# Fourteen more floats in a table of constants: where the tiles of a transformer block start in SBUF

## The chip, the cores and the metric

The kernel runs on one core of one Trainium2 chip. The metric is device time in microseconds (us) of one execution of the whole program. The kernel before was timed three times: 1037.11, 1038.47 and 1039.26 us, so its median is 1038.47 us. One more execution, of 1039.65 us, was recorded by the hardware profiler; all rows below come from that one.

## The reference, cut to what matters

One transformer block over 1024 tokens of width 1024, all in float32, and a last normalisation:

```python
h = rms_norm(x, norm_mix)
proj = h @ w_in                              # 1024 x 1536: 16 query heads, 4 key and 4 value heads of 64
mix = sliding_window_sink_attention(...)     # window 128, blocks of 128, alibi slopes, one sink per head
x = x + mix @ w_out                          # 1024 x 1024
gu = rms_norm(x, norm_ffn) @ w_gate_up       # 1024 x 5632
x = x + (silu(gu[:, :2816]) * gu[:, 2816:]) @ w_down
return rms_norm(x, final_norm)
```

Nearly all arithmetic is in four matrix products: with `w_in`, `w_out`, `w_gate_up` and `w_down`. The constants that the change is about are three small ones per partition: the exponent -0.5 for the reciprocal roots, two copies of the 16 sinks (as they are and negated), and a scale for the queries.

## The kernel before, in words

**Precision.** Every large operand is held as two float32r halves, hi (a rounded copy, made by ScalarE) and lo (the rest, a subtraction on VectorE or GpSimd). A product is three matmuls: hi with hi, hi with lo, lo with hi. A matmul has a moving operand, 128 partitions by up to 512 columns, and a stationary one, 128 by 128, which a weight load (LDWEIGHTS, engine PEld in the views) brings in ahead of it.

**Stages.** The program is one order of work written out by hand; each engine has its queue, and helpers (`Stream`, `Queue`) count matmuls and put the other engines' steps between them.

- 0 to 100 us: x is normalised and transposed into `HH` (`store`, L138); the value projection `v_mm` (L362, results in `VV`); the first half of the key and query projection (`gemm_steps`, L251), moving `HH`, stationary `wc`.
- 100 to 276 us: 32 attention units (`Unit`, L441): scores L470 and L471 (stationary `qt`, moving `KH`, `KL`), exponentials, transposes L505, values L519 (stationary `VV`, moving `pr`). Between them run the second half of L251 and then the output projection L696 (stationary `HH`, which now holds the attention output; moving `wc_o`).
- 276 to 370 us: the rest of attention and of the output projection (L732, L1073), the second normalisation, and its transposes into `HH` and `HT`.
- 370 to 808.6 us: gate and up products (`product`, L1060) in seven Strassen products for each of 22 column blocks: stationary `ws`, moving `HH` or `HT`, in groups of 12 matmuls.
- 808.6 to 987.3 us: the down projection, again in Strassen products (`d_product`, L1343): both operands are slots of `HH`, which by now holds activations and down weights; results are added into `acc`.
- 987.3 us to the end: the last columns of it, plain (L1426, both operands in `HH`), and the final norm.

**Where tiles start.** SBUF is laid out when the program is built. Pools grow from the low end (`const`, `hpool`, `vpool`, `early`, `att`, `ht`, `accp`) or, with `side="right"`, from the high end (`rows`, `wp`, `kpool`, `gp`). A tile's place is rounded up to 32 bytes. Start addresses in each partition, and what is left after division by 64:

| tile | start, bytes | remainder |
|---|---|---|
| `ident`, `small` (168 bytes, takes 192) | 16512, 17024 | 0, 0 |
| `HH` | 17216 | 0 |
| `VV`, `HT`, `acc` (the lowest of each) | 82752 | 0 |
| `wv` and the first half's `qst` | 99136, 115520 | 0 |
| attention's `dist`, `t`, `pr` | 99136, 101184, 113856 | 0 |
| `KH`, `KL` | 130912, 147296 | 32 |
| `raw_g`, `raw_s`, `sum`, `p1` (pool `gp`) | 132960 and up | 32 |
| weights: raw tiles, `wc`, `ws`, `wd` (pool `wp`) | 163680 and up | 32 |
| rows: x, `xr`, `xn`, `qt`, `gate`, `up`, `y` of the norms | 200544 and up | 32 |

Every slice that a matmul reads lies a multiple of 512 bytes from its tile's start, so the tile's remainder is the operand's. The pairs (moving, stationary) are therefore: L251 and L1060 (0, 32); L696, L732 and L1073 (32, 0); L362, L519, L1343 and L1426 (0, 0); L470 and L471 (32, 32).

The lines that the change touches are L74 to L76: the tile `small` and its slices.

Of the kernel before, what the change touches and what calls it, by code (L numbers as in the profile page):

```python
# [9 lines left out]
F32 = mybir.dt.float32  # L10
# [6 lines left out]
P = 128  # L17
# [5 lines left out]
NH = 16  # L23
# [9 lines left out]
def trunk_kernel(  # L33
# [31 lines left out]
    const = ctx.enter_context(tc.tile_pool(name="const", bufs=1))  # L65
# [5 lines left out]
    psa = ctx.enter_context(tc.tile_pool(name="psum_a", bufs=4, space=PSUM))  # L71

    ident = const.tile([P, P], F32, name="ident")
    small = const.tile([P, 2 + 2 * NH + 8], F32, name="small")  # L74
    sink_bc, sink_neg = (small[:, 2 + i * NH : 2 + (i + 1) * NH] for i in range(2))
    qscale = small[:, 2 + 2 * NH :]  # L76
    HH = hpool.tile([P, 4, 2, NK, 2 * P], F32R, name="HH")
    q_dram = [[dram.tile([P, 4, G, P], F32, name=f"qs_{i}_{kv}") for kv in range(NKV)] for i in range(2)]
    x2_dram = [dram.tile([P, D], F32, name=f"x2s_{t}") for t in range(NT)]
# [1388 lines left out]
```

## Time and profile before

| what | us |
|---|---|
| median of three runs | 1038.47 |
| profiled execution | 1039.65 |
| its span, first to last instruction | 1037.9 |
| PE (TensorE) busy with matmuls | 1000.8 (96%) |
| DVE (VectorE) busy | 643.1 (62%) |
| ACT (ScalarE) busy | 454.8 (44%) |
| POOL (GpSimd) busy | 588.9 (57%) |

A busy time is the union of the times in which an engine's instructions ran. Matmuls overlap: one is shown from its first column going in to its last result, while the next starts before that. So the time that one matmul costs is the distance between two starts, its pitch, and not its duration: a piece of the timeline with N matmuls of one kind lasts N pitches and a tail, the duration of one less its pitch. Pieces of the chain of waits have no such tail.

### The profile page before, as it was taken

The page shows a single profiled execution, that of the slowest core. Times are in us where ns is not written, and L with a number is a line of the kernel's source. Part 1 is how long each engine was busy: PE and PEld are TensorE (multiplying, and loading weights), DVE is VectorE, ACT ScalarE, POOL GpSimd, SP SyncE. Part 2 cuts the span into 40 slices and gives each one's busy share as a digit, 9 for nine tenths or more (in the row PEclk, how much of TensorE's full clock was granted, in tenths as well). Part 3 has the DMA queues.
Part 4 walks back from the last instruction along what each step waited for, and adds up shares of the span by engine and source line. Part 5 has one row for each costly group of instructions (what it writes and reads, how often), then busy time and mean ns, then how long its engine had stood idle before and what let it go on. Part 6 is the DMA issues. An engine that isn't in the chain of part 4 may idle for free.

```text
span 1037.9 us, 13830 instructions
## 1 busy us (share of the span) xinstructions
PE 1000.8 (96%) x4740; PEld 826.4 (80%) x4740; DVE 643.1 (62%) x1070; ACT 454.8 (44%) x955; POOL 588.9 (57%) x557
## 2 busy tenths in 40 slices
PE   7999999999978799999999999999999899999997
PEld 7888888888866598888888888888788688888885
DVE  5421687778886585554555455555644468886774
ACT  5533777777845443323323323323323443343334
POOL 4633555565354452663763753754743968988572
PEclk8999999999998999999999999999999999999999
DMA  8548655654355631313304413403324765343213
GB/s 271 135 123 212 153 164 133 164 191 122 105 160 140 185 103 61 132 45 126 134 24 137 145 28 126 151 20 133 132 102 138 274 266 184 109 145 108 85 41 122
DMA packets 98983, 138.28 MB, mean 133 GB/s; under 512 B 6368, under 2 KB 66784, under 8 KB 98912
## 3 DMA queue, kind: packets, MB, share of 16 engines
q1 hardware_dynamic: 98624, 136.61, 41.8%
q8 instruction: 37, 0.61, 0.2%
q10 hardware_dynamic: 288, 0.79, 0.2%
q14 instruction: 34, 0.28, 0.1%
HBM read 99.89 MB, written 35.39 MB: 130 GB/s over the span
## 4 chain that ended last, share of the span: by engine, by line
PE 63%; DMA 1%; POOL 1%; DVE 1%; ACT 0%; issue 0%; SPq 0%; POOLq 0%; DVEq 0%; ACTq 0%
PE d L1343 16%; PE gu_A L1060 12%; PE gu_B L1060 12%; PE gu_C L1060 12%; PE gu_D L1060 6%; PE dl L1426 4%; DMA acc<-x2s 1%; PE mo L1073 1%; DVE ws L925 0%; POOL sum L901 0%; POOL wc_oB L63 0%; POOL xr L641 0%; PE pt_b L620 0%; SPq L1311 0%; ACT wc_oB L60 0%
## 5 line engine op out<-in xcount | busy, mean ns | idle before, releaser
L1343 PE MATMUL d<-HH 128*128 128x512 f32 x756 | 174.8, 394 | 4.1 <-DVE acc L1354 4.1
L1343 PEld LDWEIGHTS d<-HH 128*128 128x128 f32 x756 | 143.7, 190 | 35.0 <-DVE acc L1354 4.5
L972 POOL TENSOR_TENSOR gate<-gate,up 128x512 f32<-128x512 f32 x33 | 50.4, 1529 | 162.5 <-issue 71.5
L1060 PE MATMUL gu_A<-HH,ws 128*128 128x512 f32 (+2 forms) x552 | 132.2, 388 | 0.0
L251 PE MATMUL pc<-HH,wc_c 128*128 128x512 f32 x480 | 122.0, 398 | 0.0
L1060 PEld LDWEIGHTS gu_A<-HH,ws 128*128 128x128 f32 x552 | 101.6, 188 | 22.9
L925 DVE TENSOR_TENSOR ws<-sum,ws 128x512 fp32r<-128x512 f32 x88 | 81.8, 939 | 60.8 <-ACT ws L921 60.7
L1241 POOL TENSOR_TENSOR HH<-raw_s,HH 128x512 fp32r<-128x512 f32 x63 | 92.1, 1479 | 41.8 <-ACT HH L1238 41.8
L251 PEld LDWEIGHTS pc<-HH,wc_c 128*128 128x128 f32 x480 | 87.3, 188 | 17.9
L921 ACT ACTIVATE ws<-raw_g 128x512 fp32r<-128x512 f32 x66 | 40.6, 627 | 129.6 <-issue 51.1
L921 ACT ACTIVATE ws<-sum 128x512 fp32r<-128x512 f32 x88 | 53.8, 626 | 96.5 <-POOL sum L901 61.2
L925 DVE TENSOR_TENSOR ws<-raw_g,ws 128x512 fp32r<-128x512 f32 x66 | 71.4, 1090 | 35.7 <-ACT ws L921 35.4
L496 POOL TENSOR_SCALAR t<-t,st 128x256 f32<-128x256 f32 (+1 forms) x128 | 62.7, 510 | 52.5 <-DVE st L494 32.4
L1238 ACT ACTIVATE HH<-raw_s 128x512 fp32r<-128x512 f32 x63 | 39.4, 625 | 85.0 <-PE d L1343 36.7
L1241 DVE TENSOR_TENSOR HH<-wd,HH 128x512 fp32r<-128x512 f32 x62 | 66.4, 1076 | 12.5 <-ACT HH L1238 12.5
L1354 DVE TENSOR_TENSOR acc<-d,acc 128x512 f32<-128x512 f32 x80 | 54.3, 686 | 31.5 <-PE d L1343 21.1
L483 ACT ACTIVATE t<-t,st 128x256 f32<-128x256 f32 (+1 forms) x128 | 61.9, 485 | 27.1 <-DVE st L475 27.1
L63 POOL TENSOR_TENSOR wc_c<-raw_c,wc_c 128x1024 fp32r<-128x1024 f32 x20 | 48.0, 2402 | 34.9 <-ACT wc_c L60 34.6
L1060 PE MATMUL gu_C<-HT,ws 128*128 128x512 f32 (+2 forms) x288 | 67.3, 381 | 0.0
L1060 PE MATMUL gu_D<-HT,ws 128*128 128x512 f32 (+2 forms) x276 | 66.4, 388 | 0.0
L1060 PE MATMUL gu_B<-HH,ws 128*128 128x512 f32 x264 | 65.3, 396 | 0.9 <-DVE u L1016 0.9
L1060 PE MATMUL gu_B<-HT,ws 128*128 128x512 f32 (+2 forms) x276 | 65.9, 387 | 0.0
(173 smaller groups left out, 1984.6 us busy)
## 6 DMA issues: line engine op xcount, KB each, us to landing
raw_g<-in_ffn_w_gate_up_dram SPq DMA_DIRECT2D x44, 512.0 KB, 4.1
raw_s<-actp SPq DMA_DIRECT2D x27, 512.0 KB, 3.7
wd<-in_ffn_w_down_dram SPq DMA_DIRECT2D x22, 512.0 KB, 4.8
raw_c<-in_swa_w_in_dram SPq DMA_DIRECT2D x20, 512.0 KB, 4.2
actp<-up SPq DMA_DIRECT2D x18, 512.0 KB, 5.4
qs<-qst SPq DMA_DIRECT2D x64, 128.0 KB, 2.6
qt<-qs SPq DMA_DIRECT2D x32, 256.0 KB, 4.4
actp<-gate SPq DMA_DIRECT2D x27, 256.0 KB, 4.5
```

The costliest lines, as they stand in the source:

```text
L63: lo_eng.tensor_tensor(lo, src, f(hi), ALU.subtract)
L251: nc.tensor.matmul(ps, wc[:, wl, k], hh[:, :, hl, k, :], start=(n == 0), stop=(n == 3 * NK - 1))
L483: nc.scalar.activation(self.tt[:, g, b0:], self.tt[:, g, b0:], AF.Exp, bias=st[:, 0, g : g + 1], scale=-1.0, accum_out=st[:, 3, g : g + 1],)
L496: nc.gpsimd.tensor_scalar(self.tt[:, g, b0:], self.tt[:, g, b0:], st[:, 2, g : g + 1], 0.0, ALU.mult, ALU.add)
L921: nc.scalar.activation(w[:, 0], src(), AF.Copy)
L925: nc.vector.tensor_tensor(w[:, 1], src(), f(w[:, 0]), ALU.subtract)
L972: nc.gpsimd.tensor_tensor(gate[:, s], gate[:, s], ups[kp, f_][:, s], ALU.mult)
L1060: nc.tensor.matmul(v4(ps)[:, j0:j1], w[:, wl, k], moving(i, hl, k, j0, j1), start=(first and part != "l" and n == 0), stop=(n == 11), skip ...
L1241: eng.tensor_tensor(dst[:, 1], v4(src()), f(dst[:, 0]), ALU.subtract)
L1343: nc.tensor.matmul(v4(ps), a_[:, a, j], d_[:, b], start=(first and n == 0), stop=(n == 3 * len(ps_) - 1), skip_group_check=True,)
L1354: nc.vector.tensor_tensor(dst, ps, dst, ALU.add)
L1426: nc.tensor.matmul(v4(ps), a_[:, a, t // 2], d_[:, b], start=(n == 0), stop=(n == 11))
```

## The change

`small` becomes 56 floats long instead of 42, 224 bytes instead of 168; the slice `qscale` keeps its 8 floats, and nothing reads the 14 new ones. 224 bytes are a multiple of 32, so the tile takes 224 where it took 192, and every tile of the low side behind it starts 32 bytes higher: `HH` at 17248, `VV`, `HT` and `acc` at 82784, and so on, all with remainder 32. `ident`, `small` and the high side stay where they are. The low side's highest tile then ends at 131936, below the high side's lowest at that time, 132960. No instruction is added, removed or moved.

```diff
     ident = const.tile([P, P], F32, name="ident")
-    small = const.tile([P, 2 + 2 * NH + 8], F32, name="small")
+
+    small = const.tile([P, 56], F32, name="small")
     sink_bc, sink_neg = (small[:, 2 + i * NH : 2 + (i + 1) * NH] for i in range(2))
-    qscale = small[:, 2 + 2 * NH :]
+    qscale = small[:, 2 + 2 * NH : 10 + 2 * NH]
```

## Rows read from the trace of the kernel before

**Rows 1.** Windows: stretch: length, PE, PEld, DVE, ACT, POOL busy, granted clock, DMA.
```profile
276.00:370.00 94.00, 76.35 (x358) 60.44 (x358) 67.97 (x114) 49.50 (x103) 42.48 (x53) 0.91 0.50 146
386.00:808.60 422.60, 421.70 (x1841) 340.59 (x1840) 223.78 (x270) 131.00 (x224) 227.21 (x156) 1.00 0.31 104
```

**Rows 2.** Chain of waits: start, length, what.
```profile
499.61 2.80 PE gu_C L1060 x12
...
817.58 9.79 DMA acc<-x2s
...
987.48 43.55 PE dl L1426 x192
```

**Rows 3.** Groups by form, engine PE: line, names, shape, count | busy, mean ns | idle.
```profile
L251 PE MATMUL pc<-HH,wc_c 128*128 128x512 f32 x480 | 122.0, 398 | 0.0
...
L1060 PE MATMUL gu_A<-HH,ws 128*128 128x512 f32 x504 | 124.4, 396 | 0.0
...
L1060 PE MATMUL gu_C<-HT,ws 128*128 128x512 f32 x240 | 59.2, 396 | 0.0
L696 PE MATMUL mo<-wc_o,HH 128*128 128x512 f32 x192 | 52.1, 400 | 0.0
...
L1073 PE MATMUL mo<-wc_oB,HH 128*128 128x512 f32 x96 | 31.3, 463 | 7.3 <-DVE xr L582 5.1 <-POOL wc_oB L63 1.9 <-ACT wc_oB L60 0.3
L732 PE MATMUL mo<-wc_oA,HH 128*128 128x512 f32 x96 | 26.9, 417 | 0.2 <-DVE xr L582 0.2
```

**Rows 4.** Timeline, engine PE, unbroken pieces: start, length, line, names, count.
```profile
85.83 11.36 PE L251 MATMUL pc<-HH,wc_c 128*128 128x512 f32 x48
...
899.83 30.54 PE L1343 MATMUL d<-HH 128*128 128x512 f32 x134
```

**Rows 5.** Timeline, engine PE, narrower matmuls, transposes, and L519 between others.
```profile
25.84 3.76 PE L362 MATMUL pv<-wv,HH 128*128 128x256 f32 x30
...
251.79 0.28 PE L471 MATMUL s<-KL,qt 128*128 128x256 f32 x1
...
252.51 0.28 PE L471 MATMUL s<-KL,qt 128*128 128x256 f32 x1
...
255.83 1.08 PE L519 MATMUL po<-pr,VV 128*128 128x512 f32 x4
256.75 1.32 PE L696 MATMUL mo<-wc_o,HH 128*128 128x512 f32 x5
...
260.03 1.04 PE L505 MATMUL pt<-ident,t 128*128 128x128 f32 x8
...
372.44 0.60 PE L620 MATMUL pt_b_au<-ident,xn_b 128*128 128x128 f32 x4
...
382.93 2.24 PE L1060 MATMUL gu_C<-HT,ws 128*128 128x384 f32 x12
```

**Rows 6.** Waits of engine PE: who waited for whom, us in total, times, longest.
```profile
PE mo L1073 <- DVE xr L582: 5.1, 2, 3.2
...
PE d L1343 <- DVE acc L1354: 4.1, 1, 4.1
...
PE gu_B L1060 <- DVE u L1016: 0.9, 1, 0.9
```

**Rows 7.** Groups by form, engines ACT and DVE, the splits into halves.
```profile
L921 ACT ACTIVATE ws<-raw_g 128x512 fp32r<-128x512 f32 x66 | 40.6, 627 | 129.6 <-issue 51.1 <-PE gu_A L1060 35.6 <-PE gu_C L1060 17.2
L1238 ACT ACTIVATE HH<-raw_s 128x512 fp32r<-128x512 f32 x63 | 39.4, 625 | 85.0 <-PE d L1343 36.7 <-issue 34.5 <-POOL HH L1241 9.7
...
L925 DVE TENSOR_TENSOR ws<-raw_g,ws 128x512 fp32r<-128x512 f32 x66 | 71.4, 1090 | 35.7 <-ACT ws L921 35.4
L1241 DVE TENSOR_TENSOR HH<-wd,HH 128x512 fp32r<-128x512 f32 x62 | 66.4, 1076 | 12.5 <-ACT HH L1238 12.5
```

**Rows 8.** DMA issues: names, queue, count, KB each, median us to landing.
```profile
raw_s<-actp SPq DMA_DIRECT2D x27, 512.0 KB, 3.7
...
acc<-x2s SPq DMA_DIRECT2D x8, 512.0 KB, 8.2
```

## The prediction, made before the changed kernel was built or run

> **What bounds the kernel now.** I read the windows by stage first, then the chain of waits, the groups by form, and the timeline of TensorE (PE). [...] PE waits for others only in places, above all between 276 and 370 us, where it is busy 76.35 of 94.00 us [rows 1, 6]. So the time is set by the pitch of matmuls, the distance between two starts, and whatever changes it by some ns acts thousands of times. No instruction changes here; only start addresses do, so the question is what the pitch shows of addresses.
>
> **The pitch, by pairs of remainders** (moving operand, stationary operand; all 512 columns wide unless said):
> - (0, 32): 48 matmuls of L251 last 11.36 us with a tail of 0.16 us: 11.20 / 48 = 233.3 ns [rows 4]. L1060: 2.80 / 12 = 233.3 ns [rows 2].
> - (0, 0): 134 matmuls of L1343 last 30.54 us with a tail of 0.16: 226.7 ns [rows 4]. L1426: 43.55 / 192 = 226.8 ns [rows 2].
>
> A like pair is thus 6.6 ns faster than an unlike one. It is no matter of operand shape: L251 moves two pieces of 256 columns, the products of L1060 four pieces of 128 or one of 512, and L1343 four of 128. Nor is it the clock or the work beside it, as both kinds run at full clock with the other engines half busy. In columns, 6.6 ns is little: 256 columns take 120.0 ns (3.60 / 30, L362) and 384 take 173.3 ns (2.08 / 12, L1060) [rows 5], so 128 columns cost 53.4 ns, and 6.6 ns are some 16 columns, 64 bytes of float32. That is the size of the unit that the remainders are about.
>
> Not all rows fit as neatly. The 384 columns above are an unlike pair, and 173.3 ns is just 53.4 over the like pair at 256, and 53.4 under the like pair at 512: at that width unlike costs nothing. And L519, a like pair in runs of four between unlike ones, comes at 230 ns, as 0.92 us pass from its first start to the next line's [rows 5]; a change of pair is not free at once.
>
> **The change, part by part.** It makes every 512-wide pair (32, 32).
> 1. *Gate and up, L1060, 512 wide.* The six forms hold 1776 matmuls (first and last form: 504 and 240) [rows 3]. If unlike becomes like, 1776 x 6.6 ns = 11.7 us go. What hides behind it is the feeding by the other three engines: the stage would be 2.8% shorter, and VectorE's 53.0% and GpSimd's 53.8% become 54.5% and 55.3%. One wait on VectorE of 0.9 us stands there today [rows 6]; two more such would cost 1.8 us, and that is in the range.
> 2. *Projection L251.* 480 matmuls [rows 3]: 3.2 us, half of it before 100 us, where I count it in full, 1.6 us.
> 3. *Output projection L696, L732, L1073.* 192 + 96 + 96 = 384 matmuls [rows 3]: 2.5 us.
> 4. *Values L519.* 120 matmuls of four per unit, today at 230: up to 0.4 us, once their neighbours are like pairs too.
> Of the second half of part 2, part 3 and part 4, 1.6 + 2.5 + 0.4 = 4.5 us, I count 2.0. They lie where attention's chain runs through VectorE, ScalarE and GpSimd, which the change does not hasten; what PE gains in front of a wait such as the 5.1 us on `xr` [rows 6] it spends in that wait. Bounds: 0 and 4.5.
> 5. *Down projection, L1343 and L1426, 756 + 192 = 948 matmuls.* From (0, 0) to (32, 32). No 512-wide row has that pair. Lower bound: no change. Upper: what an unlike pair costs, 948 x 6.6 ns = 6.3 us. The nearest rows are narrower: scores L471 and L470 are (32, 32) at 256 columns and take 0.72 us for six, 120 ns, the same as (0, 0) in L362 [rows 5]. I take no change.
> 6. *Transposes.* L505's operands become unlike, as `ident` stays at 0 and `t` goes to 32. L620's are that already and have (0.60 - 0.16) / 4 = 110 ns, L505's (1.04 - 0.16) / 8 = 110 ns [rows 5]: nothing.
> 7. *Splits and other steps on ScalarE, VectorE, GpSimd.* Into `HH` at 0 a ScalarE split takes 625 ns, into `ws` at 32, 627; VectorE's takes 1076 and 1090 [rows 7]. Nothing to see, and it is hidden under PE: 0, with 14 of 1090 ns (1.3%) as bound either way.
> 8. *DMAs.* `acc`, `HH`'s neighbours and the first `qst` move by 32 bytes. Weight tiles already lie at 32, and 512 KB land in `raw_s` in 3.7 us, while `acc` at 0 needs 8.2 [rows 8]; no price of 32 is to be read. The one transfer on the chain is `acc` before the second round of the down projection, 9.79 us, ended by PE's wait of 4.1 us [rows 2, 6]. Its loads go into `HT`'s place and so follow the end of gate and up, wherever that is: the wait moves along unchanged. I take 0, with 1 us either way, a tenth of that transfer.
>
> Sum: 11.7 + 1.6 + 2.0 = 15.3 us less than the profiled execution's 1039.65 us (its span 1037.9 and 1.75 around it): 1024.3 us. The three runs shown have their median 1.2 us below the profiled one, so **1023.2 us** is the forecast for a median. Its own range: 12.5 us (parts 1 and 2 less one late feed) to 17.8 us (everything) and 1 us of scatter, 1020 to 1027 us.
>
> **The rivals.**
> *A. The remainder is not what matters; no change.* L1343 and L1426 differ from the others in more than that: both their operands lie in one tile, `HH`, while the slower pairs have one on the low and one on the high side of SBUF. If nearness or the side is the cause, nothing moves: 1038.5 us. For it: L519, equal in remainder but in two tiles, has 230 and not 226.7 ns, and the unlike pair at 384 columns is free. Against it: 230 is not 233.3 either, and its runs are only four long. [...]
>
> *B. The start at 32 itself is what costs, on either operand, and two cost no more than one; slower.* Then L1060, L251 and the output projection stay at 233.3 ns, and the down projection joins them: 948 x 6.6 = 6.3 us, with L519's 120 x 3.3 ns = 0.4, so 1038.5 + 6.7 = 1045.2 us. It decides if a 512-wide (32, 32) pair has 233.3 ns. For it: every slow 512-wide pair has an operand at 32, and no row has two. Against it: at 256 columns two operands at 32 cost nothing, and at 384 one costs nothing [rows 5], which an extra piece to fetch at each crooked start would not allow.
>
> *C. Both starts at 32 add up,* 240 ns for each: (1776 + 480 + 384) x 6.6 + 948 x 13.2 ns = 29.9 us, 1068 us. Only the lack of a row leaves it open.
>
> **How the numbers follow.** My forecast gets 0.68. It explains both directions, (0, 32) and (32, 0), by one cause, and if the distance between the two starts is that cause, moving both by 32 bytes is like moving neither. A gets 0.16, B 0.13, C 0.03. A measurement of this kernel can tell about 0.2%, 2 us, from no change. Nearly all of the forecast and a little of A that is partly right make faster 0.70; A without that, 0.15; B and C with a stray 0.15 slower. The range: 1020 to 1027 leaves out a third, and B lies far off, so it reaches up to A with a little scatter: 1020 to 1040 us holds the forecast and A, 0.8.
>
> **What would show it.** Right: in the chain a gate and up product takes 2.72 us and not 2.80; 48 matmuls of L251 without a break take 11.05 us; L1343 keeps 226.7 ns; gate and up begin 1.6 to 6 us earlier and last 11.7 us less. Wrong by A: all pitches as before. Wrong by B: L1343 and L1426 at 233.3, the last 192 matmuls in 44.8 us. Wrong in size: L1060 at 226.7 ns but new waits of PE on VectorE's `ws` or on attention's steps, or the wait on `acc` longer by what was gained ahead of it.

## The result, and the profile after

The changed kernel takes 1025.96 us (median of six runs, 1022.87 to 1027.25), the kernel before 1037.86 us (six runs): ratio 0.9886, 95% interval 0.9872 to 0.9901, so 10 to 13 us faster. The forecast was 1023.2 us and the range 1020 to 1040. The profiled execution took 1025.52 us, its span 1023.7; the pair of profiled executions is 14.1 us apart, more than the medians' 11.9, because the one of before lay 1.8 us over its median and the one of after 0.4 under.

The gate and up window of the kernel after, columns as in [rows 1]; all lines of the code have moved down by one:

```profile
386.00:795.60 409.60, 408.41 (x1827) 338.77 (x1827) 228.27 (x270) 130.38 (x223) 225.92 (x155) 1.00 0.32 106
```

The chain of waits of the kernel after (start, length, what), against [rows 2]. A gate and up product has gone from 2.80 to 2.72 us, and the last 192 matmuls stand at 43.53 against 43.55:

```profile
478.80 2.72 PE gu_B L1061 x12
...
804.72 9.75 DMA acc<-x2s
...
973.37 43.53 PE dl L1427 x192
```

Its timeline on TensorE, against [rows 4]: (16.48 - 0.16) / 72 = 226.7 ns for L252, which had 233.3, and (20.56 - 0.16) / 90 = 226.7 ns for L1344, which had the same before:

```profile
83.64 16.48 PE L252 MATMUL pc<-HH,wc_c 128*128 128x512 f32 x72
...
869.62 20.56 PE L1344 MATMUL d<-HH 128*128 128x512 f32 x90
```

Where the time went is read from the first matmul of each stage, in the timelines of before and after. Before, gate and up run from 369.21 to 808.62 us, 439.4 us:

```profile
100.30 0.28 PE L470 MATMUL s<-KH,qt 128*128 128x256 f32 x1
...
369.21 2.07 PE L1060 MATMUL gu_B<-HT,ws 128*128 128x384 f32 x11
...
808.62 3.57 PE L1343 MATMUL d<-HH 128*128 128x512 f32 x15
```

After, from 367.65 to 795.64 us, 428.0 us:

```profile
99.96 0.28 PE L471 MATMUL s<-KH,qt 128*128 128x256 f32 x1
...
367.65 2.27 PE L1061 MATMUL gu_B<-HT,ws 128*128 128x384 f32 x12
...
795.64 4.70 PE L1344 MATMUL d<-HH 128*128 128x512 f32 x20
```

So 11.4 of the 14.1 us between the two executions are this one stage, 1.2 us come between 100 and 368 us (268.9 to 267.7), 0.3 before 100 us, and 1.1 in the down projection. That last 1.1 is no effect of addresses, and the 1.2 cannot be told from the scatter of single executions (both below).

The waits of TensorE after, against [rows 6]: what it waits for is what it waited for, and for about as long.

```profile
PE pt_a L136 <- DVE xn_a L126: 5.3, 2, 4.8
PE mo L1074 <- DVE xr L583: 5.0, 2, 3.3
PE d L1344 <- DVE acc L1355: 4.1, 1, 4.1
...
PE gu_B L1061 <- DVE u L1017: 1.2, 1, 1.2
```

### The profile page after: what moved, and what is told of

The parts are those of the page before. It is cut to its first block, busy times and chain, and to the rows that moved or that the text cites. A ratio compares the mean times of both kernels' runs of the same rounds, so it can differ in the third digit from the quotient of the medians.

```text
span 1023.7 us, 13830 instructions
## 1 busy us (share of the span) xinstructions
PE 985.9 (96%) x4740; PEld 825.9 (81%) x4740; DVE 646.9 (63%) x1070; ACT 454.6 (44%) x955; POOL 589.7 (58%) x557
## 4 chain that ended last, share of the span: by engine, by line
PE 62%; DMA 1%; POOL 1%; DVE 1%; ACT 0%; issue 0%; SPq 0%; POOLq 0%; ACTq 0%; DVEq 0%
PE d L1344 16%; PE gu_A L1061 12%; PE gu_B L1061 12%; PE gu_C L1061 12%; PE gu_D L1061 6%; PE dl L1427 4%; DMA acc<-x2s 1%; PE mo L1074 1%; DVE ws L926 0%; POOL sum L902 0%; POOL wc_oB L63 0%; POOL xr L642 0%; PE pt_b L621 0%; SPq L1312 0%; ACT wc_oB L60 0%
## 5 line engine op out<-in xcount | busy, mean ns | idle before, releaser
L1344 PE MATMUL d<-HH 128*128 128x512 f32 x756 | 173.5, 392 | 4.2 <-DVE acc L1355 4.1
L1344 PEld LDWEIGHTS d<-HH 128*128 128x128 f32 x756 | 142.8, 189 | 34.8 <-DVE acc L1355 4.5
L1061 PE MATMUL gu_A<-HH,ws 128*128 128x512 f32 (+2 forms) x552 | 128.9, 382 | 0.0
L926 DVE TENSOR_TENSOR ws<-sum,ws 128x512 fp32r<-128x512 f32 x88 | 84.5, 971 | 59.6 <-ACT ws L922 59.6
L252 PE MATMUL pc<-HH,wc_c 128*128 128x512 f32 x480 | 120.4, 395 | 0.0
L252 PEld LDWEIGHTS pc<-HH,wc_c 128*128 128x128 f32 x480 | 87.4, 188 | 16.6
L926 DVE TENSOR_TENSOR ws<-raw_g,ws 128x512 fp32r<-128x512 f32 x66 | 73.5, 1122 | 33.7 <-ACT ws L922 33.4
L1242 DVE TENSOR_TENSOR HH<-wd,HH 128x512 fp32r<-128x512 f32 x62 | 64.3, 1043 | 11.3 <-ACT HH L1239 11.3
```

The lines of the kernel that those rows point to most:

```text
L252: nc.tensor.matmul(ps, wc[:, wl, k], hh[:, :, hl, k, :], start=(n == 0), stop=(n == 3 * NK - 1))
L926: nc.vector.tensor_tensor(w[:, 1], src(), f(w[:, 0]), ALU.subtract)
L1061: nc.tensor.matmul(v4(ps)[:, j0:j1], w[:, wl, k], moving(i, hl, k, j0, j1), start=(first and part != "l" and n == 0), stop=(n == 11), skip ...
L1242: eng.tensor_tensor(dst[:, 1], v4(src()), f(dst[:, 0]), ALU.subtract)
L1344: nc.tensor.matmul(v4(ps), a_[:, a, j], d_[:, b], start=(first and n == 0), stop=(n == 3 * len(ps_) - 1), skip_group_check=True,)
```

## The experiments

Theory: a matmul of 512 columns is slower by 6.6 ns where its two operands start at different remainders of 64 bytes. Rivals: nearness or the side of SBUF (A), the start at 32 as such (B). e1 and e5 are small kernels that compute nothing of the block; each ran once, and all rows quoted of them lie in stretches at granted clock 1.00 (the long runs of 512 columns have there 226.7 to 234.3 ns a matmul, where a stretch of the block at 0.50 has 427).

### e1: the pitch by itself

A small kernel with operands as slices of three tiles; the offsets set the remainders (cut; one variant, which moves four pieces as the block's products do, is left out):

```python
def run(name, mov, mo, sta, so, w, n=48):          # mo, so: offsets in floats
    for i in range(n):
        a = sta[:, so + 128 * (i % 16) : so + 128 * (i % 16) + 128]
        b = mov[:, mo + 512 * (i % 4) : mo + 512 * (i % 4) + w]
        nc.tensor.matmul(ps[:, :w], a, b, start=(i == 0), stop=(i == n - 1))
run("wide_zero_near_half_wh", wide, 0, near, 8, 512)     # and so on
```

> A kernel that computes none of the reference: runs of 48 matmuls whose operands are slices of three tiles that all start at a multiple of 64 bytes; the slices' offsets set the remainders. It measures the pitch by itself. Theory (equal remainders of 64 bytes are fast): at 512 columns (0, 0) and (32, 32) have 226.7 ns, (0, 32) and (32, 0) 233.3 ns, the same whether the two tiles are neighbours or 100 KB apart; 64 bytes more on either operand change nothing. Rival A (nearness or the side of SBUF): pairs in neighbouring tiles have 226.7 and pairs far apart 233.3 ns, whatever the remainder. Rival B (a start at 32 costs): (32, 32) has 233.3 ns. At 384 columns and below the theory, by the rows of before, expects no difference; at 448 I expect half of it. Starts 8, 16, 24 or 48 bytes apart are open: between 226.7 and 233.3 ns if the price grows with the distance, 226.7 or 233.3 if it is one unit or none. Runs of five between eight transposes: about 231 ns for like and unlike pairs, as in the attention stretch.

Timeline of e1, one line for each run; a name says moving tile and its offset, stationary tile and its offset (half = 32 bytes, line = 64), and the width (wh = 512, wf = 448, we = 384); long names lack their first letters:

```profile
26.09 11.36 PE L52 MATMUL wide_zero_near_half_wh<-wide,near 128*128 128x512 f32 x48
37.28 11.36 PE L52 MATMUL wide_half_near_zero_wh<-wide,near 128*128 128x512 f32 x48
48.48 11.08 PE L52 MATMUL wide_half_near_half_wh<-wide,near 128*128 128x512 f32 x48
59.40 11.36 PE L52 MATMUL wide_zero_far_zero_wh<-wide,far 128*128 128x512 f32 x48
70.59 11.40 PE L52 MATMUL wide_zero_far_half_wh<-wide,far 128*128 128x512 f32 x48
...
104.22 11.06 PE L52 MATMUL zero_near_zero_wh_pieces<-wide,near 128*128 128x512 f32 x48
...
170.87 11.36 PE L52 MATMUL wide_zero_near_line_wh<-wide,near 128*128 128x512 f32 x48
182.07 11.40 PE L52 MATMUL zero_near_lineandhalf_wh<-wide,near 128*128 128x512 f32 x48
...
226.78 11.16 PE L52 MATMUL wide_line_near_zero_wh<-wide,near 128*128 128x512 f32 x48
...
317.92 8.51 PE L52 MATMUL wide_zero_near_zero_we<-wide,near 128*128 128x384 f32 x48
326.27 8.48 PE L52 MATMUL wide_zero_near_half_we<-wide,near 128*128 128x384 f32 x48
334.59 9.90 PE L52 MATMUL wide_zero_near_zero_wf<-wide,near 128*128 128x448 f32 x48
344.33 9.97 PE L52 MATMUL wide_zero_near_half_wf<-wide,near 128*128 128x448 f32 x48
...
374.95 8.64 PE L52 MATMUL wide_half_near_zero_we<-wide,near 128*128 128x384 f32 x48
383.43 10.07 PE L52 MATMUL wide_half_near_zero_wf<-wide,near 128*128 128x448 f32 x48
```

With the tail of 0.16 us taken off, 11.36 us are 233.3 ns, and 11.06 and 11.08 us, which hold a slower start, 227.1 and 227.5. So (32, 32) is like (0, 0) and rival B falls. At 384 columns a stationary operand 32 bytes ahead costs nothing, as the rows of before had it; but a moving operand 32 bytes ahead does. Over the last 36 pitches of each run, 384 columns have 173.3 ns like, 173.3 with the stationary and 176.7 with the moving operand ahead; 448, where I had expected half the price, have 202.7, 204.4 and 206.7 ns. Starts 8, 16, 24 and 48 bytes apart have 230.8, 233.3, 231.1 and 233.3 ns at 512 columns: two at the full price, two below it, and not in order of the distance. But two rows go against the theory: `line`, where the operands are 64 bytes apart and have equal remainders, is slow, and the two tiles far apart are slow even at (0, 0). That last looks like rival A. It isn't: the tile `far` starts 64 bytes past the others in remainders of 256, and its two rows have the very times of the two near rows with the same distance, 11.36 for `far_zero` and `near_line`, 11.40 for `far_half` and `near_lineandhalf`. (e1 has no far pair at distance 0; the kernel after and e2 have, at 2.72 us a product.) So it is low bits of the address after all, but more of them than 64 bytes need.

### e2, e3, e4: the same gain by another way, undone, and in part

e2 leaves the table alone and moves the high side down by 32 bytes; e3 does this on top of the change; e4 moves `HT` and what lies above `HH`, and not `HH`:

```diff
+    edge = ctx.enter_context(tc.tile_pool(name="edge", bufs=1, side="right"))
+    edge.tile([P, 8], F32, name="edge8")
     rows = ctx.enter_context(tc.tile_pool(name="rows", bufs=1, side="right", reuse_waits="tile"))
```
```diff
     HH = hpool.tile([P, 4, 2, NK, 2 * P], F32R, name="HH")
+    hpool.tile([P, 8], F32, name="gap8")
```

> The table of constants as before, and 8 floats put at the high end instead, so that the weights and all of the high side start 32 bytes lower, at remainder 0, like the low side at 0. Theory (equal remainders): the same gain as the change, 1024 to 1028 us (about 12 us faster), a gate and up product in 2.72 us. Rival B' (it is the low side's place at 32 that helps, or the longer table itself): no change, 1038 us, 2.80 us.

> The longer table and the 8 floats at the high end together: the low side at 32, the high side at 0, unlike again. Theory: the gain is gone, 1036 to 1040 us, products in 2.80 us, and L1344 keeps 226.7 ns. Rival B' (each shift helps by itself): 1014 to 1026 us.

> Eight floats between HH and what lies above it: HH stays at 0, HT and V go to 32, weights are at 32. Theory: within one stage, the gate and up products that move HT (744 matmuls of 512 columns) take 2.72 us, those that move HH (1032) keep 2.80 us; 744 x 6.6 ns = 4.9 us faster, 1031 to 1035 us. Rival (something that the shift does to the whole stage, such as how the feeding engines run): all products alike, 2.72 or 2.80 us.

Measured against 1038.31 us before: e2 1025.52 us, ratio 0.9877 (0.9860 to 0.9893); e3 1038.91 us, 1.0010 (0.9999 to 1.0021); e4 1033.75 us, 0.9957 (0.9942 to 0.9972). Chain of waits, e2:

```profile
504.26 2.72 PE gu_C L1062 x12
```

and e3, with the longer table in it:

```profile
504.92 2.80 PE gu_A L1063 x12
```

and e4, where products that move `HH` and products that move `HT` stand side by side:

```profile
502.24 2.80 PE gu_A L1061 x12
505.04 2.75 PE gu_D L1061 x12
507.78 2.80 PE gu_C L1061 x12
```

What helps is neither the longer table nor the place at 32: either side may be moved, and moving both gives the gain back. e4 shows the effect matmul by matmul inside one stage. Its `HT` products have 2.75 and not 2.72 us, since most of them (42 of 62) follow a slow `HH` product and need some matmuls to come to their pitch: over all 62 the first five pitches average 229.0, 232.7, 227.8, 230.5 and 229.4 ns, the sixth to eleventh 226.6 to 226.7. The first matmuls of e4's stages:

```profile
100.27 0.28 PE L471 MATMUL s<-KH,qt 128*128 128x256 f32 x1
...
367.18 2.26 PE L1061 MATMUL gu_B<-HT,ws 128*128 128x384 f32 x12
...
802.91 5.40 PE L1344 MATMUL d<-HH 128*128 128x512 f32 x23
```

Gate and up take 435.7 us where before had 439.4, so 3.7 us come from the `HT` products, of the 4.9 expected. The medians are 4.6 us apart, in range, but for a part of another kind: from 100 to 367 us e4 takes 266.9 us against 268.9, although every 512-wide pair there is as it was before. So in that stretch single executions differ by 2 us without any change of these pairs.

### e5: all distances and places

> Computes none of the reference: runs of 30 matmuls of 512 columns, the two operands in two tiles that start alike to 1024 bytes, each shifted by 0 to 224 bytes in steps of 32, all 64 pairs; ordered by the distance of the two starts, so that pairs of equal distance follow each other. e1 spoke against the first theory as a general law: 64 and 128 bytes between the starts, equal in remainders of 64, had 233.3 and 232.7 ns there. Theory now (starts must be alike in more low bits): only distance 0 of the eight has 226.7 ns for all eight places, the others 229 to 235. First theory (64 bytes): distances 0, 64, 128 and 192 have 226.7 ns, the four others 233.3. Rival (single places matter, not the distance): the pitch differs among pairs of one distance. 256 bytes more on one operand: 226.7 ns by the theory now. Starts off a 32-byte step: e1 had 231.1 for (16, 16) and 226.7 for (16, 48); I expect the same again.

Timeline of e5, runs of 30; letters a to h stand for 0 to 224 bytes in steps of 32, first of the moving operand, then of the stationary:

```profile
35.05 7.00 PE L53 MATMUL m_d_s_d<-wide,near 128*128 128x512 f32 x30
...
90.17 7.15 PE L53 MATMUL m_d_s_e<-wide,near 128*128 128x512 f32 x30
...
146.10 7.16 PE L53 MATMUL m_d_s_f<-wide,near 128*128 128x512 f32 x30
...
202.13 7.18 PE L53 MATMUL m_d_s_g<-wide,near 128*128 128x512 f32 x30
...
258.21 7.13 PE L53 MATMUL m_d_s_h<-wide,near 128*128 128x512 f32 x30
...
369.76 7.03 PE L53 MATMUL m_d_s_b<-wide,near 128*128 128x512 f32 x30
...
425.09 7.17 PE L53 MATMUL m_d_s_c<-wide,near 128*128 128x512 f32 x30
...
473.80 7.00 PE L53 MATMUL m_a_s_a_down<-wide,near 128*128 128x512 f32 x30
...
487.49 7.16 PE L53 MATMUL odd_e_e_x<-wide,near 128*128 128x512 f32 x30
494.49 7.00 PE L53 MATMUL odd_e_m_x<-wide,near 128*128 128x512 f32 x30
```

Over the last 18 pitches of each run the mean is 226.7 to 226.9 ns at distance 0, and with the stationary operand ahead by 32, 64, 96, 128, 160, 192 and 224 bytes 233.3, 233.3, 234.1 to 234.3, 232.0 to 233.3, 233.3, 228.9 and 233.4. The eight places of a distance agree to 0.2 ns, except at 128, where they alternate between 233.3 and 232.1. 256 bytes more on one operand (`_down`) are as good as none. So on a 32-byte step the pitch depends, but for that 1.3 ns, on the distance of the starts modulo 256, and only 0 is free. The first theory, with its 64 bytes, is too weak: three of its four distances cost. Off that step the rule does not hold: 16 and 16 bytes have 233.3 ns, 16 and 48 have 226.7 (the last two rows, where the letters count floats, e for 4 and m for 12). The first of these misses its expectation: e1 had 231.1 ns for 16 and 16. The two kernels place the tiles differently (their starts are alike modulo 256 bytes in e1, modulo 1024 in e5); whether that is the reason no run shows.

### e6 and e7: 64 and 256 bytes more in the kernel itself

```diff
-    small = const.tile([P, 56], F32, name="small")
+    small = const.tile([P, 72], F32, name="small")
```

This is e6; e7 has 120 in place of 72.

> The table 72 floats long: the low side 64 bytes higher than with the change, so its remainder of 64 bytes is still that of the weights (32), while the starts differ by 64. First theory (remainder of 64 bytes): as fast as the change, 1024 to 1028 us, gate and up products in 2.72 us. Theory now (alike in more low bits): the gain is gone, 1036 to 1040 us, 2.80 us; L1344 with both operands in HH keeps 226.7 ns by either.

> The table 120 floats long: the low side 256 bytes higher than with the change. Both theories: as fast as the change, 1024 to 1028 us, 2.72 us a product. If starts must be alike in still more bits (512 bytes or more): 1036 to 1040 us, 2.80 us; e1 had 226.7 ns in a pair 256 bytes apart, which speaks against this.

Measured against 1037.2 us before: e6 1029.24 us, ratio 0.9924 (0.9910 to 0.9939); e7 1026.35 us, 0.9891 (0.9873 to 0.9909). Chain of waits, e6:

```profile
504.42 2.75 PE gu_D L1061 x12
```

e6 misses both expectations and settles which of the two laws holds here: it keeps the remainder of 64 bytes and loses 2.9 of the 10.9 us that e7 gains. Its stationary operands lie 64 bytes behind the moving ones, which is 192 ahead modulo 256, and e5 has 228.9 ns for that; 12 x 228.9 ns = 2.75 us is what its products take, and its gate and up stage, 431.9 us, is 3.9 us longer than after's 428.0: 1776 x 2.2 ns. e1 had a run at that distance too, the moving operand 64 bytes ahead, 11.16 us for 48 or 229 ns; I had passed over it when I wrote the expectation.

## Why the prediction was right, point by point

**The step that carries it** (part 1) was right in mechanism and size: 11.7 us expected, 11.4 found. Feeding did not become the bound: TensorE is busy 408.41 of 409.60 us where it had 421.70 of 422.60 [rows 1], and its wait on VectorE's `u` is 1.2 us after 0.9. VectorE's share rose from 53.0 (223.78 of 422.60 [rows 1]) to 55.7% (228.27 of 409.60), to 54.6% by the shorter stage and the rest because its own work took 4.5 us more. Nearly all of that is the split into `ws`, whose 149 instructions in the stage average 1043 ns where they had 1010. Its form in [rows 7], and that of the split into `HH`:

```profile
L926 DVE TENSOR_TENSOR ws<-raw_g,ws 128x512 fp32r<-128x512 f32 x66 | 73.5, 1122 | 33.7 <-ACT ws L922 33.4
L1242 DVE TENSOR_TENSOR HH<-wd,HH 128x512 fp32r<-128x512 f32 x62 | 64.3, 1043 | 11.3 <-ACT HH L1239 11.3
```

The first took 1122 ns where it had 1090, though `raw_g` and `ws` stayed where they were; e2 has 1122 too and e3 1090 again, so in these runs it goes with the faster products and not with its own addresses. The split into `HH` went the other way, 1076 to 1043. Part 7's bound of 14 ns either way was too narrow for both; it cost nothing, as both are hidden under TensorE. Why they moved, no run shows.

**The law behind it was only half named.** The prediction took the change's own words, remainders of 64 bytes. What counts is 256: in the kernel after, `HH` at 17248 and the lowest weights at 163680 are alike even to 1024 bytes, so the change does more than it says. That is luck: the starts happened to lie 32 bytes apart modulo 256 as well. Had they lain 96 apart, the same 32 bytes would have left them 64 apart, which e5 and e6 price at 2.2 to 6.6 ns. The prediction's other hint, that 6.6 ns are 16 columns or 64 bytes, led nowhere: by e5, 64 bytes are no unit of the price. The rows of before held the hint, and I gave it another reading: L519, called a like pair, had 230 ns [rows 5]. Its operands (`pr` at 113856, `VV` at 82752) are 128 bytes apart modulo 256, before and after, so it never was like, and its 0.4 us could not come.

**Terms that were too large.** L251 before 100 us: 1.6 us expected, and from its first start (29.43 before, 30.30 after) to the first scores 70.87 us became 69.66, 1.2 us; e2 and e7 have 69.6 and 69.7, e3 71.0, so this gain comes again. The output projection, the second half of L251 and L519: 2.0 counted of 4.5, 1.2 found between 100 and 368 us, and even that is not shown to be theirs: where the pairs are alike, e2 and e7 have 266.9 and 266.5 us, but e4, with the pairs of before, has 266.9 as well. The reason is not the one I gave, waits on attention's chain, but the length of the runs. Most of these matmuls stand in runs of five, and the 153 pitches inside L696's runs average 239.7 ns before and 239.5 after: there is next to no gain that a wait could take. e1 had runs of five matmuls between eight transposes, like pairs first (397.31 to 399.35 us, 2.04 us a round) and then unlike ones (409.50 to 411.53, 2.03):

```profile
397.31 1.41 PE L61 MATMUL mixlike<-wide,near 128*128 128x512 f32 x5
...
399.35 1.40 PE L61 MATMUL mixlike<-wide,near 128*128 128x512 f32 x5
...
409.50 1.40 PE L61 MATMUL mixunlike<-wide,near 128*128 128x512 f32 x5
...
411.53 1.40 PE L61 MATMUL mixunlike<-wide,near 128*128 128x512 f32 x5
```

After each change of width the starts are irregular (in rounds two to six of like pairs the first pitch is 312 to 315 ns and the others 224 to 239; unlike pairs have 312 to 314 and 229 to 235), and five matmuls are over before the pitch settles. The prediction had that in its text ("a change of pair is not free at once") and did not use it for the sum.

**What was said to stay, stayed.** The down projection keeps 226.7 ns, which was the open bound of part 5. The wait on `acc` is 4.1 us before and after; it moved with the end of gate and up. The down projection's own length goes with the clock and not with addresses: 178.7 us before [its first start to L1426's] at a mean granted clock of 0.98, 177.6 after at 0.99, and 179.4 in e7 at 0.98, whose addresses are as good as those of after. When TensorE resumes after that wait, the granted clock is at 0.50 for a while, 5.4 us before (829.4 to 834.8) and 3.1 after (816.6 to 819.7). The 5.6 us from there on, before and after:

```profile
829.40:835.00 5.60, 5.58 (x13) 4.43 (x14) 3.56 (x6) 1.17 (x3) 1.77 (x2) 0.50 1.02 416
```
```profile
816.60:822.20 5.60, 5.59 (x18) 4.53 (x19) 3.56 (x6) 2.23 (x4) 1.78 (x2) 0.73 1.03 418
```

TensorE had stood for 4.1 us in both. Before then ran 12 matmuls at a pitch of 427 ns, after only five and one at 379, which is 1.2 us less. e7 had eight, and its wait was 5.3 us.

**What stood in the way of the rest.** Ahead of L252 the profiled execution of after lost 0.9 us (30.30 against 29.43), 0.6 of it in a wait on the first normalised rows; e7 and e2 start that line at 29.3 and 29.4 us, so this too is scatter of single executions. What the addresses are shown to give, 11.4 us in gate and up and 1.2 in L251 before 100 us, is 12.6 us and lies inside the measured 10 to 13. So nothing of the 2.0 us counted for the attention stretch need have come, and that term is the one that was too large.

**The rivals.** A is refuted by the change itself, by e1's paired rows and by e2; B by e1, e5 and the unchanged L1344, and C with it. By e5 a run's pitch depends on where the weights start against the moving operand, 226.7 to 234.3 ns. Why it does, and why at 384 columns only with the moving operand ahead (176.7 ns against 173.3, e1), no run shows; it stays open.

## What to carry to other kernels

Let the two operands of a long run of float32r matmuls of 512 columns start at the same address modulo 256 bytes, both at a multiple of 32 (226.7 to 226.9 ns a matmul, against 228.9 to 234.3 at the other distances of e5), which costs a few bytes of padding in a pool ahead of them; check the addresses after every change of a tile's size, since 32 bytes in an unrelated table are 1.1% here. Read the pitch from unbroken runs of one kind and compare it between stages: 2.80 against 2.72 us per product showed both that there was something to gain and how much. In runs of five between narrower matmuls it gave nothing (239.7 ns before, 239.5 after; in e1 2.04 us a round of like pairs, 2.03 of unlike ones). Other types of data were not run.

## What the runs showed of the hardware that I had not expected

- The period is 256 bytes (30 matmuls take 7.00 us at distance 0 and with 256 bytes more on one operand), and the price is not even within it: about 6.6 ns at most distances, 2.2 ns where the stationary operand is 192 ahead, up to 7.6 ns at 96 (e5).
- The direction counts: 64 bytes ahead 233.3 ns, 64 behind 228.9 (e5, e6).
- Equal starts off a 32-byte step are not free: 16 and 16 bytes have 233.3 ns in e5 and 231.1 in e1.
- The price goes with the width and with the operand that is moved: 32 bytes on the stationary one cost 6.6 ns at 512 columns, nothing at 480 (10.57 us for 48 like, 10.56 unlike) and 384 (173.3 ns both), and 1.7 at 448 between them; on the moving one they cost 6.6, 4.0 and 3.4 ns at 512, 448 and 384. At 256 columns the unlike pair is even the faster, 118.3 ns against 120.0 (all e1).
